# Output projection of a hybrid decoder layer: three of eight row pieces by Strassen's seven products in three column groups, GpSimd subtracting for the plain pieces

## Chip, cores and metric

The kernel runs on one core of one Trainium2 chip. The time is microseconds (us) on the device, from one launch of the whole layer; the median of three runs is given. Names of engines as the profile has them: PE is TensorE's matmuls, PEld its weight loads, DVE is VectorE, ACT ScalarE, POOL GpSimd, SP the engine that issues most DMAs.

## Reference, cut to what matters

One post-norm decoder layer on 256 positions of width 2048, all in float32. Three token mixers (gated spatial mixing, mLSTM, cross-attention) are projected to the model width, gated and summed; the sum goes through one output projection, and a LayerNorm of `ALPHA * x` plus the result follows, then a SwiGLU feed-forward with its own LayerNorm.

```python
merged = (gates[:, :, 0] * (y_a @ w_pa) + gates[:, :, 1] * (y_b @ w_pb)
          + gates[:, :, 2] * (y_c @ w_pc))
mix = merged @ w_out
x = layer_norm(ALPHA * x + mix, ln1_g[l], ln1_b[l])
x = layer_norm(ALPHA * x + swiglu_ffn(x, w_gu[l], w_down[l]), ln2_g[l], ln2_b[l])
```

The change is in the line `merged @ w_out`, a product of 256x2048 by 2048x2048.

## The kernel before

Every large product is a **job**, and a job is a row of **pieces**. A piece is 256 rows of a weight matrix by 512 of its columns, kept as one tile of 128 partitions by 1024 (two row blocks of 512 columns side by side). The list `pieces` holds all of them in one fixed order, and the main loop goes through it piece by piece; nothing else schedules the engines, each of which runs its instructions in the order in which the loop emits them.

A piece is loaded by SP (`load`, tag `raw`, 6 buffers, up to 8 pieces ahead). float32 precision is kept by splitting each operand into a high part in the fp32r format and the remainder: `split` lets ACT copy the high part (`wh`, 5 buffers, 4 pieces ahead), `split_lo` lets DVE subtract it from the raw piece (`wl`, 4 buffers, 3 pieces ahead, line 1139). Each product is then three matmuls: high by high, high by low, low by high.

Jobs of form A (weights stationary, `mul_a`, lines 1214 and 1216) give transposed results. Jobs of form B (activations stationary, weights moving, `mul_b`, lines 1179 to 1181) give rows. A plain piece of form B is 12 matmuls of 512 moving columns: two tiles of 128 positions, two row blocks, three matmuls each.

The output projection is four jobs of form B, one for each group of 512 columns, of eight pieces each (here: group 0 to 3). Groups 0 to 2 sum in one accumulator tile `acc` of two banks (psA has three such tiles); after the eighth piece `ev_out` (line 787) adds ALPHA times the residual and takes the LayerNorm statistics (line 751). Group 3 is `split`: its second tile of positions sums in two banks from the pool `psT` (tag `tr`, two buffers in all), one for each half of the columns, and its last three pieces are held back so that the LayerNorm can start early. The stationary operand, `mgT`, is written by the evacuation `ev_proj("b", j)` of the branch projection before it: each half gives one pair of row blocks, the high and low part of the merged sum (`split_from`, lines 203 and 204).

The down projection of the feed-forward already has another kind of piece. `mul_seven` (lines 1196 to 1198) does the 2x2 block product of a piece (two tiles of positions, two row blocks, two halves of columns) with seven block products in place of eight, 21 matmuls of 256 columns. It needs sums of weight blocks (`split_lo`, lines 1145 to 1150, in tags `h0` and `s5`) and sums of activation blocks (in `ev_ffup`, lines 895 to 903, run one piece later through the list `later`), and it sums two of its terms in two banks of `psT`, called c and d. `ev_seven` (lines 933 to 944) adds everything up: first the accumulator, then c and d in several steps. There the seven-product jobs are woven between pieces of form A, and the first seven-product piece of a job comes several pieces after the evacuation of the last one.

Two more names: `load_gb` loads the LayerNorm's scale and shift into tag `s5`; GpSimd has next to nothing to do (24 instructions).

Of the kernel before, what the change touches and what calls it, by code (L numbers as in the profile page):

```python
# [20 lines left out]
NT = 2  # L21
# [27 lines left out]
class Job:  # L49
    def __init__(self, form, src, act, n, evac, needs=None, bias=None, done=None, post=None, late=None, own=None, banks=False, split=False, seven=()):  # L50
        self.form = form
        self.src = src
        self.act = act
        self.n = n
        self.evac = evac
        self.needs = needs or {}
        self.post = post or {}
        self.bias = bias
        self.done = done
        self.ps = [None, None]  # L60
        self.cd = None
        self.bc = None
        self.late = late or ()
        self.own = own or {}
        self.banks = banks
        self.split = split
        self.seven = seven


class Act:  # L70
# [35 lines left out]
def layer_kernel(ctx: ExitStack, tc: tile.TileContext, xT_d, mem_d, memT_d, wi_d, wif_d, wkv_d,  # L106
# [19 lines left out]
    def slot(tag, shape, dt=F32):  # L126
        return big.tile(shape, dt, tag=tag, name=nm(tag))

    def t2(shape=None, dt=F32):
        return tmp.tile(shape or [P, 512], dt, tag="t2", name=nm("t2"))  # L130
# [16 lines left out]
    def flat(a):  # L147
        return a.rearrange("p a b -> p (a b)")
# [53 lines left out]
    def split_from(src, hi_ap, lo_ap):  # L202
        ac.activation(hi_ap, src, AF.Copy)  # L203
        ve.tensor_sub(lo_ap, src, hi_ap)
# [404 lines left out]
    def comb(job, hf, out, bias=None):  # L609
# [5 lines left out]
                ac.activation(out[:, c], ps[:, c, T:2 * T], AF.Identity, bias=pv(bias[0], bias[1] + 2 * hf + c))  # L615
        ve.tensor_add(out, out, ps[:, :, 0:T])  # L616

    def halves(f):
        def g(job):
            for hf in range(2):  # L620
                f(job, hf)
        g.half = f
        return g

    def once(key, make):
        if key not in S:
            S[key] = make()
        return S[key]
# [41 lines left out]
    def ev_proj(br, j):  # L670
        def f(job, hf):
            mg = once("mg", lambda: slot("s5", [P, KT, T]))
            kt = 4 * j + 2 * hf
            m = mg[:, kt:kt + 2]
            g = S["g" + br, j][:, 2 * hf:2 * hf + 2]
            if br == "a":
                comb(job, hf, m)
                ve.tensor_mul(m, m, g)
                return
            t = two(t2())  # L680
            comb(job, hf, t)
            ve.tensor_mul(t, t, g)
            ve.tensor_add(m, m, t)
            if br == "b":
                if "mgT" not in S:
                    m0 = slot("s3", [P, 8, 2, T], F32R)
                    S["mgT"] = Act([m0[:, 0:4], m0[:, 4:8], slot("s6", [P, 4, 2, T], F32R),
                                    slot("s6b", [P, 4, 2, T], F32R)], 4)
                mT = S["mgT"]
                split_from(m, mT.pair(kt, 0), mT.pair(kt, 1))  # L690
        return halves(f)

    def ev_zqk(h):
# [176 lines left out]
                ac.activation(g, g, AF.Silu)  # L870
        return halves(f)

    later = []

    def ev_ffup(b):
        def f(job, hf):
            g = S["hid", b][:, 2 * hf:2 * hf + 2]
            odd = b % 2
            if hf == 0:
                if odd:  # L880
                    h = slot(("s3", "s1")[b // 2 % 2], [P, 2, 2, 8, P], F32R)
                else:
                    h = slot(("s6", "s6b")[b // 2 % 2], [P, 2, 2, 2, T], F32R)
                for i in range(2):
                    S["hT", b, i] = h[:, i]
            h = S["hT", b, hf]
            u = two(t2())
            comb(job, hf, u)
            ve.tensor_mul(g, g, u)
            if h.shape[2] != 8:  # L890
                later.append(lambda: split_from(g, h[:, :, 0], h[:, :, 1]))
                return
            a = flat(g).rearrange("p (a b) -> p a b", a=4)

            def sums():
                ac.activation(h[:, 0, 0:4], a, AF.Copy)
                s = t2([P, 4, P])
                ve.tensor_tensor(s[:, 0:2], a[:, 1:2].to_broadcast([P, 2, P]), a[:, 0:4:3], ALU.subtract)
                ve.tensor_sub(s[:, 2], a[:, 0], s[:, 1])
                ve.tensor_sub(s[:, 3], a[:, 2], s[:, 2])  # L900
                ac.activation(h[:, 0, 4:8], s, AF.Copy)
                ve.tensor_sub(h[:, 1, 0:4], a, h[:, 0, 0:4])
                later.insert(0, lambda: ve.tensor_sub(h[:, 1, 4:8], s, h[:, 0, 4:8]))

            later.append(sums)
        return halves(f)

    def ev_down(b, j, first, last):
# [19 lines left out]
    def ev_seven(j, first):  # L928
        def f(job):
            a = S["acc"][:, :, j * 512:(j + 1) * 512]  # L930
            ab, (c, d) = job.ps[0], job.cd
            if first:
                ve.scalar_tensor_tensor(a, a, ALPHA, ab, ALU.mult, ALU.add)
            else:
                ve.tensor_add(a, a, ab)
            e = t2()
            ac.activation(e, d, AF.Copy)
            w, z = t2(), t2([P, 2, T])
            ve.tensor_sub(w[:, 0:T], c[:, 0:T], e[:, 0:T])
            ve.tensor_sub(w[:, T:], w[:, 0:T], e[:, T:])  # L940
            ve.tensor_tensor(z, c[:, T:].unsqueeze(1).to_broadcast([P, 2, T]), two(w), ALU.subtract)
            ve.tensor_add(a[:, 0, T:], a[:, 0, T:], c[:, 0:T])
            ve.tensor_add(a[:, 1, T:], a[:, 1, T:], w[:, T:])
            ve.tensor_add(a[:, :, 0:T], a[:, :, 0:T], z)
        return f

    def ln2(t):
# [36 lines left out]
    def J(*a, **k):  # L984
        job = Job(*a, **k)
        pieces.extend((job, i) for i in range(job.n))
# [56 lines left out]
    def sqrt_table():  # L1043
        ac.activation(pre, epst, AF.Abs_reciprocal_sqrt)

    for j in range(4):
        J("B", wout_d[j], lazy("mgT"), 8, ev_out(j), late=("out", (5, 6, 7)) if j == 3 else None, split=j == 3,
          own={6: ("s1", 0), 7: ("s1", 1)} if j == 3 else None,
          needs={0: out_start} if j == 1 else {0: sqrt_table} if j == 3 else None)

    def down(b0, nb, js=range(4)):
        for j in js:
# [80 lines left out]
    def split_lo(i):  # L1133
        l = owned.pop(i) if i in owned else wp.tile([P, 1024], F32R, tag="wl", name=nm("wl"))
        r = raw.pop(i)
        hl[i][1] = l
        job, k = pieces[i]
        if k not in job.seven:
            ve.tensor_sub(l, r, hl[i][0])  # L1139
            return  # L1140
        n7[0] += 1
        s = slot(("h0", "s5")[n7[0] % 2], [P, 2, 1024], F32R)
        hl[i].append(s)
        p, q = bc2(), bc2()
        ve.tensor_tensor(two(p), r[:, 0:T].unsqueeze(1).to_broadcast([P, 2, T]), two(r[:, T:3 * T]), ALU.add)  # L1145
        ve.tensor_add(q[:, 0:T], p[:, 0:T], r[:, 2 * T:3 * T])
        ve.tensor_add(q[:, T:], q[:, 0:T], r[:, 3 * T:])
        ve.tensor_sub(l[:, T:], r[:, T:], hl[i][0][:, T:])  # L1148
        split_from(p, s[:, 0, 0:512], s[:, 1, 0:512])
        split_from(q, s[:, 0, 512:], s[:, 1, 512:])  # L1150
# [220 lines left out]
```

## Time and profile before

| | us |
|---|---|
| median of 3 runs (lowest, highest) | 1841.02 (1840.77, 1841.02) |
| the profiled execution's own time | 1840.85 |
| its span in the trace | 1839.1 |
| PE busy | 1823.3 (99%) |
| DVE busy | 1283.1 (70%) |
| ACT busy | 945.9 (51%) |
| POOL busy | 9.5 (1%) |
| granted clock of TensorE, mean of the run | 0.998 of full speed |

The span is the part of the execution that the trace holds; the profiled execution took 1.75 us more than it. The share of an engine's busy time says how full it is; which engine sets the end is read from the chain of waits, and what a stage costs from the starts of its instructions. Matmuls are pipelined: a matmul's start to the next one's start is what it costs PE, its own duration is longer. The output projection runs from 998.24 us to about 1088 us after the span's start.

### The profile page before, as it was taken

The page shows a single profiled execution, that of the slowest core. Times are in us where ns is not written, and L with a number is a line of the kernel's source. Part 1 is how long each engine was busy: PE and PEld are TensorE (multiplying, and loading weights), DVE is VectorE, ACT ScalarE, POOL GpSimd, SP SyncE. Part 2 cuts the span into 40 slices and gives each one's busy share as a digit, 9 for nine tenths or more (in the row PEclk, how much of TensorE's full clock was granted, in tenths as well). Part 3 has the DMA queues.
Part 4 walks back from the last instruction along what each step waited for, and adds up shares of the span by engine and source line. Part 5 has one row for each costly group of instructions (what it writes and reads, how often), then busy time and mean ns, then how long its engine had stood idle before and what let it go on. Part 6 is the DMA issues. An engine that isn't in the chain of part 4 may idle for free.

```text
span 1839.1 us, 26103 instructions
## 1 busy us (share of the span) xinstructions
PE 1823.3 (99%) x10154; PEld 1575.3 (86%) x10154; DVE 1283.1 (70%) x1741; ACT 945.9 (51%) x1147; POOL 9.5 (1%) x24
## 2 busy tenths in 40 slices
PE   9999999999999999999999999999999999999997
PEld 8888888888888888888888888888888888888886
DVE  6886566557667666565555568577877878878787
ACT  6554465555555555544444355455555555555453
POOL 0000000000000000000000000000000000000001
PEclk9999999999999999999999999999999999999999
DMA  9666555555555555655556645665565565566656
GB/s 373 216 223 189 182 171 165 181 166 189 163 188 162 176 191 164 185 186 169 190 189 239 243 158 172 189 200 184 171 219 171 185 217 181 184 196 197 194 173 182
DMA packets 97627, 352.64 MB, mean 192 GB/s; under 512 B 10848, under 2 KB 11360, under 8 KB 96352
## 3 DMA queue, kind: packets, MB, share of 16 engines
q1 hardware_dynamic: 96496, 348.89, 58.5%
q0 software_dynamic: 576, 1.05, 0.5%
q8 instruction: 79, 1.29, 0.3%
q10 hardware_dynamic: 432, 1.05, 0.2%
q14 instruction: 44, 0.36, 0.1%
HBM read 348.85 MB, written 3.15 MB: 191 GB/s over the span
## 4 chain that ended last, share of the span: by engine, by line
PE 97%; DVE 2%; ACT 0%; DMA 0%; issue 0%; SPq 0%; DVEq 0%; ACTq 0%
PE acc L1214 45%; PE acc L1216 23%; PE acc L1181 7%; PE acc L1180 7%; PE acc L1179 7%; PE tr L1198 1%; PE tr L1196 1%; PE tr L1197 1%; PE acc L1198 1%; PE acc L1197 1%; PE acc L1196 1%; DVE wl L1139 1%; PE tr L198 1%; PE tr L199 0%; PE tr L200 0%; DVE t L841 0%
## 5 line engine op out<-in xcount | busy, mean ns | idle before, releaser
L1214 PE MATMUL acc<-s,wh 128*128 128x512 f32 x3520 | 966.2, 396 | 2.5 <-DVE s L846 1.1
L1139 DVE TENSOR_TENSOR wl<-raw,wh 128x1024 fp32r<-128x1024 f32 x589 | 712.3, 1222 | 362.8 <-PE acc L1216 180.9
L1120 ACT ACTIVATE wh<-raw 128x1024 fp32r<-128x1024 f32 x589 | 618.9, 1058 | 566.0 <-PE acc L1214 344.9
L1214 PEld LDWEIGHTS acc<-s,wh 128*128 128x128 f32 x3520 | 602.5, 188 | 86.6 <-DVE s L846 1.4
L1216 PEld LDWEIGHTS acc<-s,wl 128*128 128x128 f32 x3520 | 542.2, 189 | 80.9 <-DVE wl L1139 0.5
L1216 PE MATMUL acc<-s,wl 128*128 128x256 f32 x3520 | 560.8, 281 | 0.1
L1181 PE MATMUL acc<-wh,s 128*128 128x512 f32 x452 | 179.4, 397 | 0.0
L1179 PE MATMUL acc<-wh,s 128*128 128x512 f32 x452 | 179.0, 396 | 0.0
L1180 PE MATMUL acc<-wl,s 128*128 128x512 f32 x452 | 178.2, 394 | 0.0
L1181 PEld LDWEIGHTS acc<-wh,s 128*128 128x128 f32 x452 | 84.9, 188 | 20.4
L1180 PEld LDWEIGHTS acc<-wl,s 128*128 128x128 f32 x452 | 84.9, 188 | 19.4
L1179 PEld LDWEIGHTS acc<-wh,s 128*128 128x128 f32 x452 | 85.0, 188 | 18.6
L616 DVE TENSOR_TENSOR g<-g,acc 128x512 f32<-128x512 f32 x54 | 37.2, 688 | 50.3 <-ACT g L615 34.6
L615 ACT ACTIVATE g<-acc,pp 128x256 f32<-128x256 f32 x64 | 26.9, 472 | 28.9 <-PE acc L1216 28.9
L1118 ACT ACTIVATE wh<-raw 128x768 fp32r<-128x768 f32 x36 | 30.4, 845 | 18.4 <-PE acc L1214 11.7
L1181 PE MATMUL acc<-wh,s6b 128*128 128x512 f32 x96 | 38.1, 397 | 0.0
L1180 PE MATMUL acc<-wl,s6b 128*128 128x512 f32 x96 | 38.0, 396 | 0.0
L1179 PE MATMUL acc<-wh,s6b 128*128 128x512 f32 x96 | 37.8, 394 | 0.0
L612 ACT ACTIVATE t<-acc 128x512 f32<-128x512 f32 x38 | 22.7, 598 | 27.3 <-PE acc L1216 27.3
L616 DVE TENSOR_TENSOR t<-t,acc 128x512 f32<-128x512 f32 x38 | 26.1, 686 | 13.7 <-ACT t L612 13.7
L1148 DVE TENSOR_TENSOR wl<-raw,wh 128x768 fp32r<-128x768 f32 x36 | 34.3, 953 | 0.8
L203 ACT ACTIVATE s<-bc 128x512 fp32r<-128x512 f32 x36 | 22.8, 633 | 19.3 <-DVE bc L1145 15.2
(336 smaller groups left out, 1505.0 us busy)
## 6 DMA issues: line engine op xcount, KB each, us to landing
raw<-in_wi SPq DMA_DIRECT2D x238, 512.0 KB, 3.7
raw<-in_wgu SPq DMA_DIRECT2D x176, 512.0 KB, 4.2
raw<-in_wdn SPq DMA_DIRECT2D x88, 512.0 KB, 3.8
raw<-in_wkv SPq DMA_DIRECT2D x32, 512.0 KB, 3.6
raw<-in_wpb SPq DMA_DIRECT2D x32, 512.0 KB, 4.4
raw<-in_wout SPq DMA_DIRECT2D x32, 512.0 KB, 3.6
raw<-in_wpa SPq DMA_DIRECT2D x16, 512.0 KB, 3.6
raw<-in_wpc SPq DMA_DIRECT2D x16, 512.0 KB, 3.6
```

The lines of the kernel that those rows point to most:

```text
L616: ve.tensor_add(out, out, ps[:, :, 0:T])
L1120: ac.activation(h, r, AF.Copy)
L1139: ve.tensor_sub(l, r, hl[i][0])
L1148: ve.tensor_sub(l[:, T:], r[:, T:], hl[i][0][:, T:])
L1179: te.matmul(ps, a.sta(kt, 0, t), wh, start=f, stop=False)
L1180: te.matmul(ps, a.sta(kt, 0, t), wl, start=False, stop=False)
L1181: te.matmul(ps, a.sta(kt, 1, t), wh, start=False, stop=e)
L1196: te.matmul(out, a[:, 0, i], b[0], start=start, stop=False)
L1197: te.matmul(out, a[:, 0, i], b[1], start=False, stop=False)
L1198: te.matmul(out, a[:, 1, i], b[0], start=False, stop=stop)
L1214: te.matmul(ps, w[:, o:o + P], a.both(kt), start=k == 0 and j == 0, stop=False)
L1216: te.matmul(ps[:, 0:T], w[:, o:o + P], a.hi(kt), start=False, stop=k == job.n - 1 and j == 1)
```

## The change

In groups 0 to 2 the pieces 1, 3 and 6 become seven-product pieces, and the subtraction of `wl` for the other five goes from DVE to GpSimd (`aside`). Group 3 stays plain. The evacuation of groups 0 to 2 is now `ev_seven` followed by the statistics. For the three pairs 1, 3 and 6 the stationary operand is laid out in the eight blocks that `mul_seven` takes, four of them sums, made by the new `pair_sums` (the code that `ev_ffup` had); it runs through `later`, one piece after the evacuation. The weight sums of these pieces take turns in tags `h0` and `s2`, since `s5` gets the LayerNorm's scale and shift in that stage. `mgT` moves to other buffers (`s3`, `s6`, `s6b`, `s4`). No DMA is added, and SP's order is the same.

```diff
@@
+    later = []
+
+    def pair_sums(a, h):
+        ac.activation(h[:, 0, 0:4], a, AF.Copy)
+        s = t2([P, 4, P])
+        ve.tensor_tensor(s[:, 0:2], a[:, 1:2].to_broadcast([P, 2, P]), a[:, 0:4:3], ALU.subtract)
+        ve.tensor_sub(s[:, 2], a[:, 0], s[:, 1])
+        ve.tensor_sub(s[:, 3], a[:, 2], s[:, 2])
+        ac.activation(h[:, 0, 4:8], s, AF.Copy)
+        ve.tensor_sub(h[:, 1, 0:4], a, h[:, 0, 0:4])
+        later.insert(0, lambda: ve.tensor_sub(h[:, 1, 4:8], s, h[:, 0, 4:8]))
+
@@ ev_proj
-                if "mgT" not in S:
-                    m0 = slot("s3", [P, 8, 2, T], F32R)
-                    S["mgT"] = Act([m0[:, 0:4], m0[:, 4:8], slot("s6", [P, 4, 2, T], F32R),
-                                    slot("s6b", [P, 4, 2, T], F32R)], 4)
-                mT = S["mgT"]
-                split_from(m, mT.pair(kt, 0), mT.pair(kt, 1))
+                q = once("mgP", lambda: [None] * 8)
+                k = kt // 2
+                if k == 0:
+                    m3 = slot("s3", [P, 4, 2, 2, T], F32R)
+                    for i, x in enumerate((0, 2, 4, 5)):
+                        q[x] = m3[:, i]
+                    q[1], q[3] = slot("s6", [P, 2, 8, P], F32R), slot("s6b", [P, 2, 8, P], F32R)
+                    S["mgT"] = Hid(q)
+                elif k == 6:
+                    m4 = slot("s4", [P, 4096], F32R)
+                    q[6] = m4[:, 0:2048].rearrange("p (a b c) -> p a b c", a=2, b=8)
+                    q[7] = m4[:, 2048:3072].rearrange("p (a b c) -> p a b c", a=2, b=2)
+                if q[k].shape[2] == 8:
+                    later.append(lambda: pair_sums(flat(m).rearrange("p (a b) -> p a b", a=4), q[k]))
+                else:
+                    split_from(m, q[k][:, :, 0], q[k][:, :, 1])
@@
+    def ev_out7(j):
+        def f(job):
+            n = once("n1", lambda: RowNorm(S["acc"]))
+            ev_seven(j, True)(job)
+            for t in range(NT):
+                n.stats(t, j)
         return f
@@
-    for j in range(4):
+    for j in range(3):
+        J("B", wout_d[j], lazy("mgT"), 8, ev_out7(j), seven=(1, 3, 6), needs={0: out_start} if j == 1 else None)
+        pieces[-1][0].aside = (0, 2, 4, 5, 7)
+        pieces[-1][0].sums = ("h0", "s2")
+    for j in (3,):
@@ split_lo
-            ve.tensor_sub(l, r, hl[i][0])
+            (gp if k in job.aside else ve).tensor_tensor(l, r, hl[i][0], ALU.subtract)
             return
         n7[0] += 1
-        s = slot(("h0", "s5")[n7[0] % 2], [P, 2, 1024], F32R)
+        s = slot(job.sums[n7[0] % 2], [P, 2, 1024], F32R)
```

How the change moves instructions is seen at two places. First DVE at the end of group 2, before: the subtractions for the pieces ahead, then the evacuation (`s` is the residual and result, `rst` the statistics), then the next subtraction.

```order
L1139 TENSOR_TENSOR wl_9270<-raw_9176,wh_9250 128x1024
L1139 TENSOR_TENSOR wl_9288<-raw_9194,wh_9268 128x1024
L787 SCALAR_TENSOR_TENSOR s_8705<-s_8705,acc_9163 128x512
L751 BN_STATS rst_8993<-s_8705 128x6
L787 SCALAR_TENSOR_TENSOR s_8705<-s_8705,acc_9163 128x512
L751 BN_STATS rst_8994<-s_8705 128x6
L1139 TENSOR_TENSOR wl_9310<-raw_9212,wh_9286 128x1024
```

The same place after the change (c and d are both called `tr`, the scratch tiles `t`; the pieces ahead belong to group 3, which stays plain and on DVE).

```order
L1161 TENSOR_TENSOR wl_9475<-raw_9351,wh_9455 128x1024
L1161 TENSOR_TENSOR wl_9502<-raw_9380,wh_9473 128x1024
L943 SCALAR_TENSOR_TENSOR s_8717<-s_8717,acc_9338 128x2x512
L949 TENSOR_TENSOR t_9519<-tr_9357,t_9517 128x256
L950 TENSOR_TENSOR t_9519<-t_9519,t_9517 128x256
L951 TENSOR_TENSOR t_9520<-tr_9357,t_9519 128x512
L952 TENSOR_TENSOR s_8717<-s_8717,tr_9357 128x256
L953 TENSOR_TENSOR s_8717<-s_8717,t_9519 128x256
L954 TENSOR_TENSOR s_8717<-s_8717,t_9520 128x2x256
L775 BN_STATS rst_9081<-s_8717 128x6
L775 BN_STATS rst_9082<-s_8717 128x6
L1161 TENSOR_TENSOR wl_9533<-raw_9398,wh_9500 128x1024
```

The accumulator is still read first; bank c (`tr_9357`) is read for the last time by the fifth instruction of the evacuation, line 952 of the changed kernel (line 942 of the kernel before).

Second, PE at the end of group 2 and the start of group 3 after the change (`acc_9338` is the accumulator of group 2, `acc_9536` that of group 3, `tr_9543` and `tr_9544` are its two banks from `psT`).

```order
L1203 MATMUL acc_9338<-wh_9400,s_8861 128x512
L1201 MATMUL acc_9536<-wh_9437,s_7699 128x512
L1202 MATMUL acc_9536<-wl_9457,s_7699 128x512
L1203 MATMUL acc_9536<-wh_9437,s_7699 128x512
L1201 MATMUL acc_9536<-wh_9437,s_7699 128x512
L1202 MATMUL acc_9536<-wl_9457,s_7699 128x512
L1203 MATMUL acc_9536<-wh_9437,s_7699 128x512
L1201 MATMUL tr_9543<-wh_9437,s_7699 128x256
L1202 MATMUL tr_9543<-wl_9457,s_7699 128x256
```

The order is that of the kernel before; what is new is that `tr_9543` takes the buffer in which group 2 kept c, so that six matmuls of group 3 stand between group 2's last matmul and the next need of that bank.

## Rows read from the trace of the kernel before

**Rows 1.** The page's part 4, chain of waits of the whole span, by engine and line.
```profile
PE 97%; DVE 2%; ACT 0%; DMA 0%; issue 0%; SPq 0%; DVEq 0%; ACTq 0%
PE acc L1214 45%; PE acc L1216 23%; PE acc L1181 7%; PE acc L1180 7%; PE acc L1179 7%; PE tr L1198 1%; PE tr L1196 1%; PE tr L1197 1%; PE acc L1198 1%; PE acc L1197 1%; PE acc L1196 1%; DVE wl L1139 1%; PE tr L198 1%; PE tr L199 0%; PE tr L200 0%; DVE t L841 0%
```

**Rows 2.** Timeline (start, length in us), PE: first matmuls of column groups 0, 1, 2.
```profile
998.24 0.39 PE L1179 MATMUL acc<-wh,s 128*128 128x512 f32 x1
...
1020.65 0.39 PE L1179 MATMUL acc<-wh,s 128*128 128x512 f32 x1
...
1043.05 0.39 PE L1179 MATMUL acc<-wh,s 128*128 128x512 f32 x1
```

**Rows 3.** Timeline, PE: first matmul of a seven-product piece, and of the piece behind.
```profile
1201.03 0.28 PE L1196 MATMUL tr<-wh,s 128*128 128x256 f32 x1
...
1203.54 1.09 PE L1214 MATMUL acc<-s,wh 128*128 128x512 f32 x4
```

**Rows 4.** Groups of DVE instructions, shapes apart: count, busy us, mean ns, idle before.
```profile
L1139 DVE TENSOR_TENSOR wl<-raw,wh 128x1024 fp32r<-128x1024 f32 x589 | 712.3, 1222 | 362.8 <-PE acc L1216 180.9 <-issue 108.5 <-PE acc L1180 47.6
...
L1148 DVE TENSOR_TENSOR wl<-raw,wh 128x768 fp32r<-128x768 f32 x36 | 34.3, 953 | 0.8
...
L1145 DVE TENSOR_TENSOR bc<-raw 128x512 f32<-128x512 f32 x36 | 24.7, 685 | 0.0
...
L204 DVE TENSOR_TENSOR s<-bc,s 128x512 fp32r<-128x512 f32 x36 | 23.2, 684 | 0.0
...
L1146 DVE TENSOR_TENSOR bc<-bc,raw 128x256 f32<-128x256 f32 x36 | 15.3, 426 | 1.2
...
L944 DVE TENSOR_TENSOR s<-s,t 128x512 f32<-128x512 f32 x18 | 12.4, 686 | 0.0
...
L940 DVE TENSOR_TENSOR t<-t,t 128x256 f32<-128x256 f32 x18 | 7.7, 425 | 0.6
```

**Rows 5.** Timeline, PE and DVE: a seven-product job's evacuation beside the next piece.
```profile
1220.13 1.08 PE L1214 MATMUL acc<-s,wh 128*128 128x512 f32 x4
1220.33 1.22 DVE L933 SCALAR_TENSOR_TENSOR s<-s,acc 128x1024 f32<-128x1024 f32 x1 [0.35 <-PE acc L1181]
...
1222.98 0.41 DVE L942 TENSOR_TENSOR s<-s,tr 128x256 f32<-128x256 f32 x1
...
1223.65 0.69 DVE L944 TENSOR_TENSOR s<-s,t 128x512 f32<-128x512 f32 x1
```

**Rows 6.** Timeline, DVE: the last step of the evacuation before the output projection.
```profile
1003.94 0.69 DVE L204 TENSOR_TENSOR s6b<-s,s6b 128x512 fp32r<-128x512 f32 x1 [0.70 <-ACT s6b L203]
```

**Rows 7.** Groups of DVE and ACT instructions, shapes apart: activation sums and weight copies.
```profile
L1120 ACT ACTIVATE wh<-raw 128x1024 fp32r<-128x1024 f32 x589 | 618.9, 1058 | 566.0 <-PE acc L1214 344.9 <-PE acc L1181 108.9 <-issue 65.9
...
L901 ACT ACTIVATE s<-t 128x512 fp32r<-128x512 f32 x10 | 6.3, 634 | 32.8 <-DVE t L900 32.8
...
L898 DVE TENSOR_TENSOR t<-g 128x256 f32<-128x256 f32 x10 | 4.2, 419 | 0.0
L899 DVE TENSOR_TENSOR t<-g,t 128x128 f32<-128x128 f32 x10 | 2.9, 292 | 0.3
```

**Rows 8.** Groups of POOL instructions: busy us, mean ns, idle before.
```profile
L978 POOL TENSOR_TENSOR s<-s,s 128x512 f32<-128x512 f32 x1 | 1.3, 1267 | 3.6 <-ACT s L974 3.6
...
L171 POOL TENSOR_SCALAR_AFFINE_SELECT upper<-ones 128x128 f32<-128x128 f32 x1 | 0.3, 294 | 0.0
...
L170 POOL MEMSET epst<- 128x1 f32 x1 | 0.1, 99 | 0.0
```

**Rows 9.** Timeline, DVE and POOL: a subtraction beside GpSimd's one wide instruction.
```profile
123.90 1.21 DVE L1139 TENSOR_TENSOR wl<-raw,wh 128x1024 fp32r<-128x1024 f32 x1
...
123.97 2.10 POOL L300 TENSOR_SCALAR_AFFINE_SELECT wT<-wT 128x1024 f32<-128x1024 f32 x1 [121.04 <-DMA wT<-in_gws]
```

**Rows 10.** PE's longest pause behind the output projection (timeline).
```profile
1093.00 1.20 PE L1214 MATMUL acc<-s,wh 128*128 128x512 f32 x4 [1.06 <-DVE s L846]
```

**Rows 11.** Busy us of PE, PEld, DVE, ACT, POOL around it, clock, DMA share, GB/s.
```profile
1088.00:1096.00 8.00, 6.60 (x46) 5.46 (x45) 5.90 (x16) 5.58 (x10) 0.00 (x0) 1.00 0.00 0
```

More of the change, by code (lines that the diff above doesn't have):

```diff
@@ L67, in __init__ @@
         self.seven = seven
+        self.aside = ()
+        self.sums = ("h0", "s5")
 class Act:
@@ L871, in ev_ffgate @@
         return halves(f)
-    later = []
     def ev_ffup(b):
@@ L892, in f @@
                 return
[L893 to L905, printed above, removed]
+            later.append(lambda: pair_sums(flat(g).rearrange("p (a b) -> p a b", a=4), h))
         return halves(f)
@@ L944, in f @@
             ve.tensor_add(a[:, :, 0:T], a[:, :, 0:T], z)
+        return f
+    def ev_out7(j):
[4 more added lines that the diff above has]
+                n.stats(t, j)
         return f
@@ L1044, in sqrt_table @@
         ac.activation(pre, epst, AF.Abs_reciprocal_sqrt)
-    for j in range(4):
+    for j in range(3):
[3 more added lines that the diff above has]
+    for j in (3,):
         J("B", wout_d[j], lazy("mgT"), 8, ev_out(j), late=("out", (5, 6, 7)) if j == 3 else None, split=j == 3,
           own={6: ("s1", 0), 7: ("s1", 1)} if j == 3 else None,
-          needs={0: out_start} if j == 1 else {0: sqrt_table} if j == 3 else None)
+          needs={0: sqrt_table} if j == 3 else None)
     def down(b0, nb, js=range(4)):
```

## The prediction

> **What bounds the kernel now.** The chain of waits comes first: it lies on PE for 97% of the span [rows 1], and the lines of the output projection (1179 to 1181) have 7% each of it. So a microsecond taken from PE's matmuls is a microsecond of the whole, as long as PE finds its operands and its banks ready. Next the timeline of PE in this stage: group 0 starts at 998.24, group 1 at 1020.65, group 2 at 1043.05 [rows 2]. Groups 1 and 2 lie 22.40 apart, eight pieces of 2.80, with no pause between the groups: PE never waits here today. Third, the groups of DVE instructions by shape give the price of what is added, and the timeline of one seven-product evacuation the order in which it lets its banks go.
>
> **What PE saves.** A seven-product piece runs from 1201.03 to 1203.54, 2.51 us [rows 3]; a plain one costs 2.80. Nine pieces save 9 x 0.29 = 2.6 us. This is the whole possible gain, 0.14% of the time. That the piece is one eighth shorter in matmul columns would give 0.35; the shorter matmuls give a sixth of that back.
>
> **Bank c between groups.** The first seven-product piece of a group is piece 1, and its first three matmuls start bank c anew. The two banks of `psT` are all there are, so PE must wait until the evacuation of the group before has read c for the last time (line 942, line 952 after the change). In the down projection's evacuation the first instruction starts 0.20 after the next piece's first matmul (1220.33 against 1220.13), and line 942 ends at 1222.98 + 0.41 = 1223.39, so c is free 3.26 us after PE has gone on [rows 5]. There, several pieces come in between and nobody waits. Here, at the ends of groups 0 and 1, one plain piece of 2.80 stands in between: PE waits 0.46, say 0.5, twice. At the end of group 2 it is worse: group 3 is split, and after six matmuls of its piece 0 (half a plain piece, 1.40) it starts its first half bank, which is the buffer of c. PE waits 3.26 - 1.40 = 1.9 us. Together 2.9 us. Before, these waits do not exist. What could make them longer is DVE arriving late at the evacuation. By row it does not: in a group DVE has for each of the three seven-product pieces 0.69 + 2 x 0.43 + 0.95 + 2 x 0.68 = 3.9 [rows 4], 11.6 in all, and an evacuation from 1220.33 to 1223.65 + 0.69, 4.0 [rows 5], besides the statistics that it has today; that is 15.6 in a group of 5 x 2.80 + 3 x 2.51 = 21.5, and the eight subtractions of 1.22 that it does now are gone. The last sums before an evacuation belong to the next group's piece 1 and can start when piece 5 is done, 5.3 us before it.
>
> **GpSimd's subtractions.** The trace has no GpSimd instruction of this shape. Bounds: from above, twice the one with two inputs at half the width, 2 x 1.27 = 2.53 [rows 8]; from below, the one-input instruction of this width, 2.10 [rows 9]. I take 2.4, nearest to the former because it has two inputs too, less a little since a fixed part is paid once. A group has five, 12.0 us of 21.5. Each may start three pieces ahead, some 8 us, so mostly they are hidden. The tight place is piece 5 of group 0. The evacuation of branch b ends today at 1003.94 + 0.69 = 1004.6 [rows 6]; one of its two splits (a subtraction of 0.69 and 0.70 of waiting for ScalarE) moves behind, so 1003.2. Then DVE makes the sums of piece 3, about 3.7 with their overlap, until 1006.9, and the first three sums of pair 6, 0.42 + 2 x 0.29, until 1008.0; ScalarE copies them, 0.63, and only then the high part of piece 5, 1.06, until some 1009.7 [rows 7]; GpSimd's 2.4 end at 1012.1. PE has pieces 0 to 4 behind it after 3 x 2.80 + 2 x 2.51 = 13.4, and wants the low part at its second matmul, 998.24 + 13.4 + 0.2 = 1011.9. A wait of 0.2; with the bounds, none to 0.3.
>
> **What is hidden.** The activation sums of pairs 1 and 3 fall into the branch projections, where DVE idles 0.6 us on the average before each subtraction [rows 4] and has pieces of 2.8 to fill; if that cover were gone, each would cost at most its own 2.4 us. ScalarE's extra copies are hidden in its idle half (it is busy 51% of the span). SP's order is unchanged; a raw buffer is let go about 1.2 us later, with six buffers and loads up to eight pieces ahead. The statistics, the x1 chain behind group 3 and the stages after it keep their work. PE's new pauses stay under 2 us; around today's pause of 1.06 the granted clock is 1.00 [rows 10, 11], so I cost the clock at nothing.
>
> **The sum.** -2.6 + 2.9 + 0.2 = +0.5 us. The profiled execution took 1840.85, so 1841.4; the median of the three runs stands 0.2 above that execution, so 1841.5. The change gives PE less to do and makes it wait for it.
>
> **The rivals.**
>
> *The two engines hinder each other in SBUF (slower).* DVE's weight sums and remainders read two inputs from SBUF, and so does each GpSimd subtraction. If such instructions exclude each other, a group has 11.6 + 0.43 + 0.42 + 0.69 = 13.1 us of them on DVE (the last three are the evacuation's lines 940, 943, 944 [rows 4]) and 12.0 on GpSimd, 25.1 against 21.5 of PE: 3.6 too many, 11 us over three groups. Worse, DVE then comes to the evacuation late, by about one instruction of each engine, 2.4 to 3 us at each of two or three ends, and bank c with it: up to 18. Less the saving that is in the sum already, 1841.5 + 14.5 = 1856. It decides as soon as the two sums pass PE's 21.5. Rows: GpSimd's one wide instruction ran from 123.97 for 2.10, and a DVE subtraction from 123.90 for 1.21, as short as the usual 1.22 [rows 4, 9]. Eight times the 128-wide one alone, 0.29, would be 2.35 [rows 8], so nothing looks delayed. But if most of those 0.29 is a fixed part (the smallest memset takes 0.10), the work alone may be near 1.0, and 1.1 of waiting may be in the 2.10. So the rows leave it open. Chance 0.30.
>
> The Trainium skill (SBUF — State Buffer, section Who interferes with whom) states just this: a VectorE instruction with two SBUF inputs contends with a GpSimd instruction that reads SBUF, and the one that starts second is blocked until the first is done. By that rule the time would be the 1856 of this rival; the subtraction that began at 123.90 shows no sign of being held, GpSimd's row beside it can be read both ways, and no run here settles it yet.
>
> *GpSimd is only slower than its rows (slightly slower).* At 3.6 us instead of 2.4 the wait at piece 5 of group 0 grows by 1.2, 1842.7; at 5.0 five of them need 25 in a group of 21.5 and add 3.5 in each of the last two, some 1850. For it speaks that DVE is busy beside them; against, the 2.10 of [rows 9]. Chance 0.10, 1842.5 to 1850.
>
> *The banks do not bind (faster).* If the evacuation lets c go before PE wants it, or PE has the waits filled elsewhere, only the saving is left: 1841.0 - 2.6 = 1838.4; with half the waits 1839.9. Against it stands the order of the evacuation [rows 5]: c is read last in its fifth instruction, and the first one needs the group's last matmul. Chance 0.10.
>
> That the nine pieces are not shorter is hardly possible: 36 such pieces run in the down projection with the same matmuls.
>
> **How the numbers follow.** Forecast 0.50, with its own range 1840.5 to 1842.5; GpSimd and DVE excluding each other 0.30; GpSimd slower 0.10; banks not binding 0.10. 0.2% is 3.7 us, about what a measurement of this kernel can surely tell from no change. Faster than that is out of reach of a saving of 2.6; I leave 0.03 for what the trace does not show. Slower by more: the first rival and half of the second, 0.35. Within: 0.62. The range from 1838.8 to 1856.0 takes in the forecast, the second rival, most of the third and half of the first.
>
> **What would show it.** Nine pieces of 2.51 on PE; waits on PE for DVE's line 952 of about 0.5, 0.5 and 1.9 at the starts of piece 1 of groups 1 and 2 and of the first half bank of group 3; GpSimd's fifteen subtractions at about 2.4 with DVE's durations unchanged. Group 1 would then be 22.0 long. Wrong would be: DVE subtractions well over 1.22 or gaps between them without a releaser while GpSimd runs, PE waiting for POOL at many pieces, or the evacuation beginning more than 0.3 after the group's last matmul.

## The result and the profile after

| | before | after |
|---|---|---|
| median of 4 runs each (lowest, highest), us | 1841.02 (1840.77, 1841.26) | 1853.53 (1853.18, 1854.19) |
| the profiled execution, us | 1840.85 | 1853.36 |
| its span, us | 1839.1 | 1851.5 |
| granted clock of TensorE, mean of the run | 0.998 | 0.996 |

The change makes the kernel slower by 12.5 us: the ratio to before is 1.0068, with a 95% interval of 1.0051 to 1.0086. That lies inside the predicted range, but not where the forecast put it (1841.5). It is near what the first rival gave (1856).

The page of the changed kernel: busy time by engine, the chain of waits by engine, and from the costliest groups the row of GpSimd's new subtractions.

```profile
PE 1826.2 (99%) x10235; PEld 1581.1 (85%) x10235; DVE 1324.5 (72%) x1798; ACT 954.7 (52%) x1171; POOL 48.3 (3%) x39
...
PE 93%; DVE 5%; ACT 1%; issue 0%; DMA 0%; ACTq 0%; DVEq 0%
...
L1161 POOL TENSOR_TENSOR wl<-raw,wh 128x1024 fp32r<-128x1024 f32 x15 | 38.9, 2603 | 445.0 <-DVE bc L1169 405.3
```

The chain lay on PE for 97% and on DVE for 2% [rows 1]; now DVE has 5% of it. GpSimd's fifteen subtractions took 2.60 us on the average, against the 2.4 that I had taken from the bounds of [rows 8, 9]; the first two, which ran before the stage began, took 2.40 each. So GpSimd itself was as fast as foretold. The average over the whole span hides the rest: the shares have to be read in the stage.

**Where the time went.** Windows of the changed kernel, one row for each of column groups 0, 1 and 2, from the first matmul of the group to the first of the next (length, then busy us of PE, PEld, DVE, ACT, POOL with counts, granted clock, DMA share, GB/s):

```profile
997.98:1022.94 24.96, 22.31 (x126) 18.71 (x125) 23.79 (x26) 11.64 (x16) 12.07 (x5) 1.00 0.41 131
1022.94:1050.20 27.26, 23.51 (x125) 20.10 (x124) 26.95 (x28) 11.22 (x15) 14.16 (x6) 0.94 0.68 245
1050.20:1076.48 26.28, 23.32 (x125) 20.05 (x123) 24.16 (x29) 12.27 (x16) 7.81 (x3) 0.94 0.56 171
sum 78.50, PE 69.14 PEld 58.86 DVE 74.90 ACT 35.13 POOL 34.05; mean PE 23.05 PEld 19.62 DVE 24.97 ACT 11.71 POOL 11.35
```

The same windows of the kernel before:

```profile
998.24:1020.65 22.41, 22.41 (x99) 18.02 (x98) 14.30 (x16) 9.92 (x11) 0.00 (x0) 1.00 0.56 187
1020.65:1043.05 22.40, 22.40 (x98) 18.02 (x97) 12.27 (x12) 8.52 (x8) 0.00 (x0) 1.00 0.76 285
1043.05:1065.45 22.40, 22.40 (x98) 18.02 (x97) 12.27 (x12) 8.51 (x8) 0.00 (x0) 1.00 0.54 184
```

Before, PE is busy throughout and DVE for little more than half. After, the groups are 25.0, 27.3 and 26.3 us long and DVE is busy for 95, 99 and 92% of them. Three groups take 78.50 instead of 67.21, 11.3 more; another 1.0 is a wait in group 3, below. So in this stage the bound has passed from PE to DVE. The prediction had given DVE 15.6 us a group besides the statistics; 24 to 27 is far from it.

**Why DVE is full.** Groups of DVE instructions of the changed kernel, shapes apart, in the output projection (count, busy us, mean ns, idle before): the three weight sums of a seven-product piece, and line 950, the first step of the evacuation with both inputs in SBUF (953 and 954, the other two, come later and kept their 0.42 and 0.69).

```profile
L1168 DVE TENSOR_TENSOR bc<-bc,raw 128x256 f32<-128x256 f32 x9 | 16.3, 1816 | 0.3
L1167 DVE TENSOR_TENSOR bc<-raw 128x512 f32<-128x512 f32 x9 | 15.0, 1667 | 0.0
...
L1169 DVE TENSOR_TENSOR bc<-bc,raw 128x256 f32<-128x256 f32 x9 | 5.9, 657 | 0.3
...
L950 DVE TENSOR_TENSOR t<-t,t 128x256 f32<-128x256 f32 x3 | 4.5, 1492 | 0.1
```

By [rows 4] the same instructions take 0.685 (512 wide) and 0.425 (256 wide). The excess is 9 x 1.39 + 9 x 0.98 + 9 x 0.23 + 3 x 1.07 = 26.6 us. It shows nowhere as a wait: the profile counts a held instruction as busy. Which ones are held, the timeline of DVE and POOL at the end of group 0 shows (start, length):

```profile
1018.47 5.41 POOL L1161 TENSOR_TENSOR wl<-raw,wh 128x1024 fp32r<-128x1024 f32 x2 [2.03 <-DVE s L206]
...
1018.72 2.90 DVE L1167 TENSOR_TENSOR bc<-raw 128x512 f32<-128x512 f32 x1
1021.65 2.52 DVE L1168 TENSOR_TENSOR bc<-bc,raw 128x256 f32<-128x256 f32 x1
1024.20 0.42 DVE L1169 TENSOR_TENSOR bc<-bc,raw 128x256 f32<-128x256 f32 x1
...
1026.61 1.21 DVE L943 SCALAR_TENSOR_TENSOR s<-s,acc 128x1024 f32<-128x1024 f32 x1
...
1027.59 2.35 POOL L1161 TENSOR_TENSOR wl<-raw,wh 128x1024 fp32r<-128x1024 f32 x1 [3.70 <-ACT wh L1142]
...
1027.74 0.42 DVE L949 TENSOR_TENSOR t<-tr,t 128x256 f32<-128x256 f32 x1
1028.20 2.02 DVE L950 TENSOR_TENSOR t<-t,t 128x256 f32<-128x256 f32 x1
...
1030.86 0.41 DVE L952 TENSOR_TENSOR s<-s,tr 128x256 f32<-128x256 f32 x1
```

Two GpSimd subtractions run from 1018.47 to 1023.88. The two DVE sums that begin in that time take 2.90 and 2.52 instead of 0.69 and 0.43, 2.2 and 2.1 more, most of a GpSimd instruction each; the second ends at 1024.17, 0.29 after the pair. The third, behind it, is short again. At 1027.74 line 949, with one input in PSUM, runs its usual 0.42 beside GpSimd; line 950 behind it, with both inputs in SBUF, ends at 1030.22, 0.28 after GpSimd.

**What PE then waits for.** Waits of PE in the stage (engine and line, releaser: us in total, times, longest):

```profile
PE tr L1218 <- DVE s L952: 6.0, 2, 3.1
PE tr L1219 <- DVE wl L1170: 1.9, 2, 1.1
PE acc L1236 <- DVE s L870: 1.2, 1, 1.2
PE tr L1201 <- DVE s L952: 1.0, 1, 1.0
PE acc L1202 <- POOL wl L1161: 0.8, 1, 0.8
PE tr L1218 <- ACT t L947: 0.7, 1, 0.7
```

The third was there before [rows 10]. The others are new, 10.4 us. The largest are two pauses of 3 us for the bank that the group before had as c, whose last reader, line 952, stands in DVE's queue behind the held sums and the held line 950. Behind these two pauses the clock falls. The timeline of PE, group 1:

```profile
1027.97 0.28 PE L1220 MATMUL tr<-h,s 128*128 128x256 f32 x1
1031.33 0.58 PE L1218 MATMUL tr<-h,s 128*128 128x256 f32 x1 [3.08 <-DVE s L952]
1031.70 0.41 PE L1219 MATMUL tr<-h,s 128*128 128x256 f32 x1
1031.92 0.41 PE L1220 MATMUL tr<-h,s 128*128 128x256 f32 x1
...
1034.69 0.40 PE L1201 MATMUL acc<-wh,s 128*128 128x512 f32 x1
1034.93 0.39 PE L1202 MATMUL acc<-wl,s 128*128 128x512 f32 x1
```

For 3 us after the pause, 256-column matmuls start 0.21 apart instead of 0.12, which is the lower of the two clock levels, 1.2 for 2.4 GHz. The mean clock of groups 1 and 2 is 0.94, as the windows above show. By the starts of the matmuls the two stretches at the lower clock are 1.6 and 1.5 us longer than at the upper one; whether that is a loss of its own is asked in E9.

### The profile page after: what moved, and what is told of

Its sections match the earlier page's. It is cut to its first block, busy times and chain, and to the rows that moved or that the text cites. A ratio compares the mean times of both kernels' runs of the same rounds, so it can differ in the third digit from the quotient of the medians.

```text
span 1851.5 us, 26367 instructions
## 1 busy us (share of the span) xinstructions
PE 1826.2 (99%) x10235; PEld 1581.1 (85%) x10235; DVE 1324.5 (72%) x1798; ACT 954.7 (52%) x1171; POOL 48.3 (3%) x39
## 3 DMA queue, kind: packets, MB, share of 16 engines
q8 instruction: 80, 1.31, 0.3%
## 4 chain that ended last, share of the span: by engine, by line
PE 93%; DVE 5%; ACT 1%; issue 0%; DMA 0%; ACTq 0%; DVEq 0%
PE acc L1236 44%; PE acc L1238 23%; PE acc L1203 6%; PE acc L1201 6%; PE acc L1202 6%; PE tr L1218 1%; PE tr L1220 1%; PE tr L1219 1%; PE acc L1220 1%; PE acc L1219 1%; PE acc L1218 1%; DVE bc L1168 1%; DVE wl L1161 1%; DVE bc L1167 1%; PE tr L200 1%; DVE s L206 1%
## 5 line engine op out<-in xcount | busy, mean ns | idle before, releaser
L1161 DVE TENSOR_TENSOR wl<-raw,wh 128x1024 fp32r<-128x1024 f32 x565 | 683.5, 1222 | 334.5 <-PE acc L1238 179.2
L1142 ACT ACTIVATE wh<-raw 128x1024 fp32r<-128x1024 f32 x580 | 608.3, 1056 | 529.0 <-PE acc L1236 346.3
L1201 PE MATMUL acc<-wh,s 128*128 128x512 f32 x438 | 174.7, 399 | 0.0
L1202 PE MATMUL acc<-wl,s 128*128 128x512 f32 x438 | 173.6, 396 | 0.8 <-POOL wl L1161 0.8
L1203 PE MATMUL acc<-wh,s 128*128 128x512 f32 x438 | 174.1, 398 | 0.0
L1161 POOL TENSOR_TENSOR wl<-raw,wh 128x1024 fp32r<-128x1024 f32 x15 | 38.9, 2603 | 445.0 <-DVE bc L1169 405.3
L1140 ACT ACTIVATE wh<-raw 128x768 fp32r<-128x768 f32 x45 | 37.8, 841 | 20.5 <-PE acc L1236 11.4
L205 ACT ACTIVATE h<-bc 128x512 fp32r<-128x512 f32 x44 | 27.8, 632 | 37.0 <-DVE bc L1167 25.6
L1170 DVE TENSOR_TENSOR wl<-raw,wh 128x768 fp32r<-128x768 f32 x45 | 42.9, 953 | 3.6 <-PE acc L1238 2.9
L205 ACT ACTIVATE s<-bc 128x512 fp32r<-128x512 f32 x46 | 27.7, 623 | 29.4 <-DVE bc L1167 19.7
L1167 DVE TENSOR_TENSOR bc<-raw 128x512 f32<-128x512 f32 x45 | 39.7, 882 | 0.0
```

What stands on the lines that cost most here:

```text
L1140: ac.activation(h[:, T:], r[:, T:], AF.Copy)
L1142: ac.activation(h, r, AF.Copy)
L1161: (gp if k in job.aside else ve).tensor_tensor(l, r, hl[i][0], ALU.subtract)
L1201: te.matmul(ps, a.sta(kt, 0, t), wh, start=f, stop=False)
L1202: te.matmul(ps, a.sta(kt, 0, t), wl, start=False, stop=False)
L1203: te.matmul(ps, a.sta(kt, 1, t), wh, start=False, stop=e)
```

## The experiments

Three theories stood against each other. **A:** GpSimd's subtractions and DVE's instructions with two inputs in SBUF exclude each other, and that makes DVE the bound. **B:** the seven-product pieces themselves cost it, by DVE's added work and the bank waits. **C:** GpSimd is too slow for its own five pieces. All ratios are to runs of the kernel before on the same chip.

**E1: the plain pieces' subtractions back on DVE.**

```diff
-        pieces[-1][0].aside = (0, 2, 4, 5, 7)
```

> The nine seven-product pieces stay, all subtractions go back to DVE. Theory A (GpSimd's subtractions and DVE's two-input instructions exclude each other): DVE has 3 x 3.6 + 5 x 1.13 + 5.2 = 21.6 us a group against PE's 21.5, just full, and its instructions have their usual lengths again (0.69, 0.43): 1842, between 1839.5 and 1844. Theory B (the seven-product pieces themselves cost it, by DVE's extra work and the waits for banks): DVE now has still more to do, 1853 or above. Theory C (GpSimd is too slow for its own pieces): as A, 1842.

Measured: 1842.02 (1841.21 to 1842.24, 10 runs), ratio 1.0006 (0.9997 to 1.0015). Groups of DVE instructions, the first two of the three sums (one line earlier here; the third has the mean of the second) and the evacuation's line 950:

```profile
L1166 DVE TENSOR_TENSOR bc<-raw 128x512 f32<-128x512 f32 x9 | 6.1, 681 | 0.0
L1167 DVE TENSOR_TENSOR bc<-bc,raw 128x256 f32<-128x256 f32 x9 | 3.8, 425 | 0.3
...
L950 DVE TENSOR_TENSOR t<-t,t 128x256 f32<-128x256 f32 x3 | 1.3, 425 | 0.1
```

Waits of PE in the same kernel:

```profile
PE tr L1200 <- DVE s L952: 1.0, 1, 1.0
PE tr L1218 <- DVE wl L1169: 0.4, 1, 0.4
```

The durations are back to normal and the 12.5 us are gone, all but about one. Giving DVE fifteen subtractions more (15 x 1.22 = 18.3 us) makes the kernel faster, because it takes 26.6 us of holding away. B falls as an account of the 12.5. What it does account for is that the saving is gone here too: E1 stands 4.0 above the 1838.0 that its 2.7 us of saving alone would give, with DVE nearly full and short waits for low parts, and with one bank wait of 1.0 at group 3, not three of 2.9 in sum.

**E2: GpSimd's subtractions alone, no seven-product pieces.** The kernel before, with the same fifteen pieces on GpSimd.

```diff
...
+        if j < 3:
+            pieces[-1][0].aside = (0, 2, 4, 5, 7)
...
-            ve.tensor_sub(l, r, hl[i][0])
+            (gp if k in job.aside else ve).tensor_tensor(l, r, hl[i][0], ALU.subtract)
```

> The kernel before, with the same fifteen subtractions on GpSimd and no seven-product piece. Theory A: DVE has only three subtractions a group left and much idle time; those that fall beside GpSimd become up to 2.4 us longer, PE hardly notices: 1841 to 1842. Theory B: 1841, and nothing longer. Theory C: PE waits for GpSimd at pieces 5 and 0 of the groups, 1845 or above.

Measured: 1840.70 (1840.42 to 1841.85, 10 runs), ratio 0.9999 (0.9990 to 1.0009). Groups of DVE and POOL instructions (the subtractions of the plain pieces, in the first three groups):

```profile
L1142 DVE TENSOR_TENSOR wl<-raw,wh 128x1024 fp32r<-128x1024 f32 x18 | 23.8, 1326 | 38.9 <-PE acc L1183 29.6 <-PE acc L1219 7.6 <-PE acc L1184 1.1
...
L1142 POOL TENSOR_TENSOR wl<-raw,wh 128x1024 fp32r<-128x1024 f32 x15 | 39.4, 2641 | 432.5 <-PE acc L1219 408.5 <-PE acc L1184 7.1 <-issue 7.0
```

GpSimd is as slow here as in the changed kernel (2.64), and PE has no new wait. C falls. The holding is there too, both ways: DVE's mean is 1.33 instead of 1.22, and two GpSimd subtractions in a row that began just behind one of DVE's took 5.73 instead of 2 x 2.40 (timeline of DVE and POOL):

```profile
1023.11 1.21 DVE L1142 TENSOR_TENSOR wl<-raw,wh 128x1024 fp32r<-128x1024 f32 x1
...
1023.22 5.73 POOL L1142 TENSOR_TENSOR wl<-raw,wh 128x1024 fp32r<-128x1024 f32 x2 [3.29 <-PE acc L1184]
```

But DVE was busy for only 37.6 of 90 us around the stage, so no engine had to wait for the held instructions.

**E3: GpSimd writes the same tiles, at about the same length, and reads nothing.** The low part of fifteen pieces is left out.

```diff
+            if k in job.aside:
+                gp.memset(l.bitcast(F32), 0.0)
+                gp.memset(l.bitcast(F32), 0.0)
...
```

> The change, but GpSimd fills the fifteen low parts with zeros, twice each (about 2 x 0.96 us), and reads nothing; the low parts of these pieces are left out of the product. Theory A, if only reads of SBUF exclude: DVE's 0.69 and 0.43 come back, 1839.6 (1839 to 1841), the saving of 2.6 less one wait of 1.2 at group 3. Theory A, if any GpSimd access excludes: DVE is held for 0.96 to 1.9 at a time, 1845 to 1850. Theory B: 1852 to 1854.

Measured: 1839.86 (1839.04 to 1840.29, 10 runs), ratio 0.9994 (0.9985 to 1.0004). Windows of the three groups:

```profile
997.90:1019.41 21.51, 21.51 (x126) 18.80 (x125) 17.22 (x30) 13.28 (x19) 9.51 (x10) 1.00 0.56 176
1019.41:1040.91 21.50, 21.50 (x125) 18.80 (x124) 15.97 (x27) 11.11 (x15) 9.49 (x10) 1.00 0.83 314
1040.91:1062.41 21.50, 21.50 (x125) 18.80 (x124) 15.92 (x24) 10.70 (x13) 5.68 (x6) 1.00 0.56 186
```

Groups of DVE instructions, the first two sums, and a place on the timeline where one runs beside a memset:

```profile
L1171 DVE TENSOR_TENSOR bc<-raw 128x512 f32<-128x512 f32 x9 | 6.1, 682 | 0.0
...
L1172 DVE TENSOR_TENSOR bc<-bc,raw 128x256 f32<-128x256 f32 x9 | 3.8, 425 | 0.3
...
1012.31 0.96 POOL L1163 MEMSET wl<- 128x1024 f32 x1
...
1012.54 0.68 DVE L1171 TENSOR_TENSOR bc<-raw 128x512 f32<-128x512 f32 x1
```

This is the stage as the forecast had it, but for the bank waits. GpSimd writes into SBUF for 24.7 us in the three groups, at places right beside DVE's sums, and these keep their 0.68 and 0.43. A group takes 21.50 and DVE is busy for 16 to 17 us of it. DVE runs the same program as in the changed kernel (81 of its instructions fall into these windows, 83 into the others), and needs 49.1 us for the three groups instead of 74.9: by the windows the holding cost it 25.8, close to the 26.6 from the durations.

**E4: GpSimd reads one input instead of two.** It copies the raw piece in place of the subtraction, so the low part of these pieces is not the remainder.

```diff
+            if k in job.aside:
+                gp.tensor_copy(l, r)
...
```

> The change, but GpSimd copies the raw piece into the low part, so that it reads one input and not two; the subtraction of the high part is left out for these fifteen pieces. Theory A: DVE is held for as long as a copy takes, 1 to 2 us, and the time lies between, 1842 to 1850. If only GpSimd instructions with two inputs exclude DVE: 1839.6 and DVE's usual lengths. Theory B: 1852 to 1854.

Measured: 1842.71 (1841.94 to 1844.52, 10 runs), ratio 1.0010 (1.0001 to 1.0020). Timeline of POOL and DVE at one such copy:

```profile
1012.29 1.04 POOL L1162 CAST wl<-raw 128x1024 fp32r<-128x1024 f32 x1 [2.94 <-issue]
...
1012.30 1.31 DVE L1172 TENSOR_TENSOR bc<-bc,raw 128x256 f32<-128x256 f32 x1
```

One input is enough: a sum of 0.43 waits out the copy of 1.04. The holding is as long as GpSimd's instruction, so with copies of 1.14 on the average it is less than half of what it was each time, 6.8 us in all against E3's durations, and DVE mostly keeps up.

The Trainium skill (SBUF — State Buffer, section Who interferes with whom) has just this rule: a VectorE instruction with two SBUF inputs contends with a GpSimd instruction that reads SBUF, not with one that only writes it. The runs agree in each part: 2.52 for 0.43 beside a subtraction, 1.31 beside a copy, 0.43 on the average in E3. Line 949, which has only one input in SBUF, kept its 0.42 beside a subtraction.

**E5: zeros in the pauses, a miss.** The question was whether the low clock is a loss of its own. Matmuls of zeros, which add nothing to the sums, were put ahead of the first product that needs bank c.

```diff
+WD = 24
...
+        if first and S.get('n1'):
+            for _ in range(WD):
+                te.matmul(ab[:, 0, 0:P], zero, ones, start=False, stop=False)
```

> The change, with 24 matmuls of a zero tile (128 columns each, about 2.9 us) put on PE just ahead of the first product that waits for bank d in groups 1 and 2, where the changed kernel has its two pauses of 3 us; they add nothing to the sums. If the two pauses cost more than their own length because PE runs at half the clock behind them (1.4 and 1.6 us by the starts of the matmuls behind them), the time falls from 1853.5 to 1850.5. If the clock behind the pauses costs nothing on the path, it stays at 1853.5 or rises a little.

Measured: 1951.09 (1950.85 to 1951.27, 4 runs), ratio 1.0598. The condition also held for the seven-product jobs of the down projection, 18 of them, and a zero matmul cost 0.23, not 0.12: 24 of them fill 5.5 us where the pause has 3. The time says nothing on the question. The clock was 1.00 in both groups, so work in the pause does keep it up. E9 repeats this properly.

**E6: the banks read out early.** The changed kernel, but c and d are read right after piece 6, before the sums of the next pieces.

```diff
...
+            ve.scalar_tensor_tensor(a, a, ALPHA, job.ps[0], ALU.mult, ALU.add)
+            ve.tensor_add(a[:, 0, T:], a[:, 0, T:], y[:, 0:T])
...
+        pieces[-1][0].post = {6: (lambda jb: lambda: ev_banks(jb))(pieces[-1][0])}
```

> The change with the subtractions still on GpSimd, but c and d are read out right behind the last seven-product piece of a group, one plain piece before the accumulator, and their last terms are kept in SBUF; the sums stay the same. Theory A: the pauses at the banks (7.7 us with group 3's) go for the most part, but DVE is still held by GpSimd and PE then waits for its weight sums: 1848 to 1851. If the banks alone were the cause: 1840 to 1841.

Measured: 1851.06 (1850.30 to 1851.93, 4 runs), ratio 1.0054 (1.0040 to 1.0068). The first wait of PE in its list:

```profile
PE tr L1236 <- DVE wl L1187: 6.8, 4, 2.7
```

Of the waits for a bank one of 0.8 is left (for line 965, now the last reader of c), but 6.8 us for the low parts of seven-product weights have come, and only 2.5 of 12.5 us are gained. The bank pauses were the place where DVE's lateness came out, not its cause.

**E7 and E8: no GpSimd, banks early, two or three pieces of eight.** E8 has the three seven-product pieces of the change, E7 two, with pair 3 of the stationary operand in the plain layout; all subtractions are on DVE, and both read c and d as E6 does. E7's edit:

```diff
...
-        J("B", wout_d[j], lazy("mgT"), 8, ev_out7(j), seven=(1, 3, 6), needs={0: out_start} if j == 1 else None)
-        pieces[-1][0].aside = (0, 2, 4, 5, 7)
+        J("B", wout_d[j], lazy("mgT"), 8, ev_out7(j), seven=(1, 6), needs={0: out_start} if j == 1 else None)
...
```

> No subtraction on GpSimd, two seven-product pieces a group (1 and 6), c and d read out early. Theory A: DVE has 2 x 3.6 + 6 x 1.13 + 5.2 = 19.2 us in a group of 22.0, no wait on PE is left but those of the kernel before, and six pieces save 6 x 0.29 = 1.7: 1839.0 to 1839.3. If DVE or the banks still bind with two pieces: 1840 or above.

> No subtraction on GpSimd, three seven-product pieces a group as in the change, c and d read out early. DVE is full (21.6 us in a group of 21.5) and PE waits now and then for its weight sums, 1 to 2.5 us in all; the wait for a bank at group 3 goes against the run with all subtractions on DVE: 1840.2 to 1841.0, between that run's 1842.0 and the 1839.1 that is expected with two pieces a group.

Measured: E7 1839.78 (1839.10 to 1841.67, 11 runs), ratio 0.9994 (0.9985 to 1.0003); E8 1840.83 (1840.14 to 1840.98, 11 runs), ratio 0.9998 (0.9989 to 1.0007). With two pieces PE has no new wait at all; its span is 1837.6 against 1839.1, close to the 6 x 0.29 = 1.7 that six pieces save. With three, DVE is busy for 24.55 of the 25 us from 1025 on, PE waits 0.9 and 0.4 for its low parts, and the span is only 0.6 shorter, of 2.6. Both intervals include 1: neither beats the kernel before by more than the measurement can tell.

**E9: zeros in the pauses, rightly placed.** As E5, with 12 matmuls, in groups 1 and 2 of the output projection alone.

```diff
+WD = 12
...
+        pieces[-1][0].fill = j > 0
...
+        if first and job.fill:
+            for _ in range(WD):
+                te.matmul(ab[:, 0, 0:P], zero, ones, start=False, stop=False)
```

> The changed kernel, with 12 matmuls of zeros (0.23 each, some 2.8 us) put in front of the first product that needs the late bank, in column groups 1 and 2 of the output projection alone; they add nothing to the sums and lie where PE paused for 3.08 and 2.96 us. If the half clock behind these pauses is a loss of its own (about 3.0 us), it goes: 1850.5, with a mean granted clock of 1.00 in both groups and 512-column matmuls 0.23 apart behind. If the clock only shows what the waits cost anyway, the time stays at 1853.5. 1856 or more if the zeros do not lie inside the pause.

Measured: 1853.65 (1852.38 to 1855.11, 4 runs), ratio 1.0072 (1.0055 to 1.0089). Windows of groups 1 and 2:

```profile
1022.92:1049.36 26.44, 24.96 (x149) 21.44 (x148) 26.13 (x28) 11.22 (x15) 13.44 (x6) 1.00 0.68 242
1049.36:1075.58 26.22, 24.95 (x149) 21.44 (x148) 25.02 (x29) 12.24 (x16) 8.56 (x4) 1.00 0.50 173
```

Waits of PE:

```profile
PE tr L1223 <- DVE wl L1174: 2.7, 4, 1.1
...
PE tr L1222 <- ACT t L950: 1.1, 2, 0.7
```

The zeros lay inside the pauses, with 0.4 us of waiting for line 955 (line 952 of the changed kernel) left behind each, and the clock is 1.00. But the median has not moved: the second of the outcomes on record. The first, 1850.5, would be a ratio of 1.0052 to the changed pair's 1841.0, just below the measured interval. By its own profile this run is 1.0 us shorter than that of the changed kernel (1852.38 against 1853.36), within the spread of its four runs. Where PE is faster after the pause, it waits sooner for the next low part (2.7 in all instead of 1.9) and the next bank (1.1 instead of 0.7). The half clock of the changed kernel ran while DVE set the pace, so it was mostly a symptom: by the profiles it is worth about 1 us, and the times cannot tell 1 from nothing.

## Why the prediction came out as it did

**The saving** was right: 3 x (22.40 - 21.50) = 2.7 us in E3, 2.6 foretold, and a seven-product piece in the changed kernel still takes 2.51 from its first matmul to the next piece's.

**Bank c** was mis-sized, 2.9 for 1.0. I let a group's c follow the c of the group before, and the text on the change, like the prediction, let group 3's first half bank take c. The traces say otherwise: the first product of a group, into c, waits for ScalarE's copy of the old d (line 947, 0.7), and the fifth, into d, for line 952, the last reader of the old c. So the banks change places from group to group, and what PE wants first is the one that is let go first. The fifth product starts 12 x 0.12 = 1.44 later than the first, 2.80 + 1.44 = 4.24 after the last group's matmuls, and bank c is free after 3.26 [rows 5]: no wait in groups 1 and 2. In group 3 the first half bank goes without a wait, and it is the second, six shorter matmuls (0.72) later, that waits for line 952. By the row that leaves 3.26 - 1.40 - 0.72 = 1.1, and 1.0 was measured in E1, E3 and the changed kernel alike (timeline of PE, changed kernel):

```profile
1079.80 0.39 PE L1201 MATMUL tr<-wh,s 128*128 128x256 f32 x1 [1.05 <-DVE s L952]
```

The evacuation's order of steps and their lengths, on which the step also stood, were right where nothing was held.

**GpSimd's low part** was nearly right: one wait of 0.8 where I had 0.2, at the second matmul of piece 5 of group 0, the place foretold. Its subtraction began at 1011.35 instead of 1009.7, because DVE's sums ahead of it had been held. Its price of 2.4 was right where nothing held it.

**The forecast's failed step** is the assumption that the prices of DVE and GpSimd add nothing to each other: that DVE's durations stay as in [rows 4]. In fact DVE's sums and line 950 took 26.6 us more than by those rows, and the three groups took 14.0 more than in E3, where nothing is held. The stated range holds the result only because it was wide enough for half of the first rival; the forecast's own, 1840.5 to 1842.5, missed it by 11 us. The first rival, given 0.30, is what happened. Its working comes close in the first group: 25.1 us of excluding work where PE has 21.5, and the group took 24.96. That it is so close is in part luck, since the 25.1 counts the evacuation of a group, and none falls into that window. The next two took 27.26 and 26.28, with the late evacuation and a bank pause of 3.1 and 3.0 in each, which that rival had as 2.4 to 3. Together: -2.7 for the saving, +14.0 for three groups of 78.50 against the 64.51 of E3, +1.0 for the bank at group 3, is +12.3; the profiled executions differ by 12.5. The 14.0 are the new waits inside these groups, 9.4, and 4.6 more of busy time for the same 376 matmuls (69.14 against 64.51 in E3), of which the lower clock is some 3. The rival's 1856 was 2.5 too high, but that nearness is partly luck, as its 14.5 is not the sum of its terms: 11 and two or three late ends of 2.4 to 3 are 15.8 to 20, and the saving, which 1841.5 holds already, was taken off a second time. By its own terms it would have been 1857.3 to 1861.5, and 1.9 of that is what it took over too much with the bank term.

**The clock** I had costed at nothing, since PE's pauses were to stay under 2 us. They reached 3.1 and the clock did fall, but E9 shows that this was not what the time was made of.

**How the evidence could have been weighed.** [Rows 9] was read both ways, and I gave more weight to the DVE subtraction that was not held. But DVE began first there, at 123.90, and GpSimd 0.07 later. Of two instructions that exclude each other the second waits, so the row that could show it was GpSimd's 2.10. A one-input GpSimd copy of that width that came first took 1.04 in E4; 2.10 is 1.06 more, and DVE's subtraction had 1.14 still to run. E2 shows the same order: DVE first, at 1023.11, with its usual 1.21, and GpSimd from 1023.22 with 0.93 too much. This fits exclusion; that the instruction of [rows 9], a select, takes as long as a copy when it is alone was not measured.

**The other rivals.** GpSimd's own speed was no part of it (E2). That the banks do not bind was mostly right: without the holding they bind at group 3 alone, for 1.0 (E3).

## What to carry to other kernels

Before moving work from one engine to another to relieve it, check whether the two may run beside each other at all: here 18.3 us taken off DVE put 26.6 us of holding on it. A profile counts a held instruction as busy, so compare its mean duration with the same shape elsewhere, and test with a variant that writes without reading. When a resource that paces a stage is late, removing the waits where it shows (a bank, a clock) moves them to the next place; only its own work counts.

## What the runs showed of the hardware

DVE instructions with two SBUF inputs and GpSimd instructions that read SBUF excluded each other for the whole length of the one that was first: 2.52 for 0.43 beside a subtraction of 2.5. GpSimd is held as well: two subtractions took 5.73 instead of 4.80. A memset of the same 128x1024 tile (0.96) held nothing.

Behind pauses of PE of 3.08 and 2.96 us the granted clock fell to its lower level for about 3 us, the second time only after 1 us at full clock (starts 0.12 apart to 1058.49, then 0.43 for 512 columns to 1061.83); behind the pause of 1.06 it stayed at 1.00 [rows 11], and zero matmuls in the pause kept it there. A float32 matmul of 128 columns appears twice in the trace and cost 0.23 us, as much as one of 512 in the fp32r format.
